# Second layer's rotated scores: query parts stacked on 128 partitions, two passes in place of three

## The chip, the cores and the metric

The kernel runs on one core of a Trainium2 chip, as one program of some 27,500 instructions on five engines: TensorE (PE in the profile; its weight loads are listed apart as PEld), VectorE (DVE), ScalarE (ACT), GpSimd (POOL) and SyncE (SP), which issues the loads of weights. The metric is the device time of one execution in microseconds (us); lower is better.

## The reference, cut to what matters

The reference is a block of two layers followed by a second block. The first layer's mixer is a gated delta rule, the second layer's is latent attention (MLA) of 256 tokens over 512 keys, 256 of the context and 256 of the sequence itself; the second block has sparse, dilated and cross attention and an MLP. All numbers are float32. The change touches the latent attention only:

```
z_lat = h_lat @ w_in                       # 384 query, 256 key/value, 64 rotary columns
ckv, kr = split(kv_part, [256])            # kr: 64 columns, shared by all 8 heads
kv = (rms_norm(ckv, g) @ w_ukv)            # per head: kn (128) and v (128)
q  = (rms_norm(cq, g) @ w_uq)              # per head: qn (128) and qr (64, rotated)
s  = einsum('bqhd,bkhd->bhqk', qn, kn) + einsum('bqhd,bkd->bhqk', qr, kr)
p  = softmax(s * 192 ** -0.5)
o  = einsum('bhqk,bkhd->bqhd', p, v)
y  = o @ w_out
```

The rotation (`rot`) is applied to qr and to the 256 keys of the sequence; the keys of the context are taken as they are.

## The kernel before, in words

**Three passes for a product.** Every float32 operand of a product is split into a high part, rounded to TensorE's input type (F32R in the code), and a low part, the remainder; ScalarE writes the high part (line 344) and VectorE the low one (line 345), in `split`. A product is then three passes of TensorE over the same accumulator: high by high, low by high, high by low (`mm3`, line 368; the fourth is left out). All passes are issued by line 366, so that the profile has them under one line and tells them apart by their tiles.

**The second layer** (`layer1`, line 1429) comes about half way through. First the keys' and queries' inputs are projected and normalised. The rotary key part is a tile `kz` of 128 partitions in which the same 64 rows stand twice (the weight columns are doubled on the host); its first 256 columns (context) are split as they are, the others after `rope` (line 1388), into `krh` and `krl`. Then come the values (`w_uv`), the rotary query parts (`ev_qr`, line 1490: for each pair of heads one tile of 128 partitions, even head on the lower 64, odd head on the upper 64, rotated and split into `qrh` and `qrl`), and, head by head, the plain query and key parts (`qk`, line 1499).

**The loop over the 8 heads** (line 1509) does for each head: the `qk` of the next head (15 passes), and for each of two tiles of 128 queries the scores of 512 keys in one PSUM bank `ps_s`: three passes with `qn`/`kn` over 128 rows and three with `qr`/`kr` over the 64 rows of this head. Then softmax (line 1406: maximum on VectorE, exponential on ScalarE, reciprocal and product on VectorE), four transposes of the result into `ps_pt`, a split of them, and 12 passes with the values into `ps_po`. There are two banks for `ps_s`, two for `ps_mm`, two for `ps_pt` and one for `ps_po`.

**What sets the order.** The instructions are recorded in program order, and a scheduler then places them on each engine by priorities and its own estimate of when each is ready; it puts passes of several heads between each other. Each engine works through its own list in that order and waits at the first instruction whose inputs are not there. Loads of weights are issued by SyncE in one queue (line 350) into a ring of buffers.

Of the kernel before, what the change touches and what calls it, by code (L numbers as in the profile page):

```python
# [10 lines left out]
F32 = mybir.dt.float32  # L11
F32R = mybir.dt.float32r
I32 = mybir.dt.int32
AF = mybir.ActivationFunctionType
ALU = mybir.AluOpType
# [4 lines left out]
P = 128  # L20
# [242 lines left out]
class K:  # L263
# [1121 lines left out]
        x["DT"] = DT  # L1385


    def rope(self, pool, z, rot, srot, cos, sin, hi, lo, T=256):

        nc = self.nc  # L1390
        p1 = self.sm()
        n = z.shape[0]
        self.mm(p1[:, :T], srot[:n], z, True, True)
        a = self.t(pool, [P, 256], "ra", 2)
        b = self.t(pool, [P, 256], "rb", 2)
        if rot is None:
            nc.gpsimd.tensor_tensor(a, z, cos, op=ALU.mult)
        else:
            p2 = self.sm()
            self.mm(p2[:, :T], rot[:n], z, True, True)  # L1400
            nc.vector.tensor_tensor(a, p2[:, :T], cos, op=ALU.mult)
        nc.vector.tensor_tensor(b, p1[:, :T], sin, op=ALU.mult)
        nc.vector.tensor_tensor(a, a, b, op=ALU.add)
        self.split(a, hi, lo)

    def softmax(self, pool, ps, n, scale, bias=None, w=256):
# [22 lines left out]
    def layer1(self):  # L1429
        nc, d = self.nc, self.d  # L1430
        m = self.mods[1]
        halves = ((0, 256), (256, 512))
        with ExitStack() as es:
            pool = es.enter_context(self.pool("mla"))
            c2 = self.consts(pool, "c2")
            qch, qcl = self.pair(pool, [P, 3, 256], "qc")
            ckh, ckl = self.pair(pool, [P, 2, 512], "ck")
            krh, krl = self.pair(pool, [P, 512], "kr")
            with self.pool("mla_l", side="right") as lp, self.pool("mla_h", side="right") as hp:
                A = self.scales(1, 1, "n1_1")  # L1440
                hl, bcs, ends = [], [], ()
                for h in (1, 0):
                    self.nrt = NRT[h]
                    hl.append(self.pair((hp, lp)[h], [P, 8, 258], f"h{h}"))
                    bcs.append(self.prepb(lp, [self.x[:, k, 256 * h:256 * h + 256] for k in range(8)],
                                          lambda k: A[:, k, 1 - h:2 - h], m[:, 0:8, 1 - h:2 - h], *hl[-1], soon=h == 1))
                    ends = ends or (self.rooted, self.spread)

                def ev(dst, ps, i):

                    b = self.t(hp, [P, 1], "zb", 4)
                    nc.vector.tensor_copy(b, ps[:, 256:257])
                    nc.vector.tensor_tensor(dst, ps[:, :256], bcs[i], op=ALU.mult)
                    nc.scalar.activation(dst, dst, AF.Identity, bias=b)

                def both(chunks, dst):

                    ws = [[w.rearrange("p (k m) -> p k m", k=8) for w in self.chunk(ap)] for ap in chunks]
                    for i, o in ((0, 256), (1, 0)):
                        for j, (wh, wl) in enumerate(ws):  # L1460
                            ps = self.ps()
                            for k in range(8):
                                self.mm3(ps[:, :258], (wh[:, k], wl[:, k]), (hl[i][0][:, k], hl[i][1][:, k]), k == 0, k == 7)
                            ev(dst(j)[:, o:o + 256], ps, i)
                cz = self.t(hp, [P, 2, 512], "cz")
                both([d["w_mc"][j] for j in range(2)], lambda j: cz[:, j])
                self.nrt = NRT[2]
                self.norm(hp, [cz[:, j] for j in range(2)], 512, lambda k, h: self.v("mkg", k),
                          None, ckh, ckl, ((0, 512),))
                kz = self.t(hp, [P, 512], "kz")  # L1470
                both([d["w_mkr"][0]], lambda j: kz)
                self.split(kz[:, :256], krh[:, :256], krl[:, :256])
                self.rope(pool, kz[:, 256:], None, c2["perm64"], c2["axc"], c2["axs"], krh[:, 256:], krl[:, 256:])
                qz = self.t(hp, [P, 3, 256], "qz")
                with self.behind(*ends):
                    self.gemm([d["w_mq"][j] for j in range(3)], 8, P, *hl[0], 258, lambda j, ps: ev(qz[:, j], ps, 0))
                self.nrt = NRT[3]
                self.norm(hp, [qz[:, j] for j in range(3)], 256, lambda k, h: self.v("mqg", k),
                          None, qch, qcl, ((0, 256),))
                self.nrt = "nr"  # L1480
                self.fill(FILL[0])
            self.mo = self.pool("mla_o", side="right")
            pool = self.mo.__enter__()
            oh, ol = self.pair(pool, [P, 8, 256], "o")
            tmp = self.pool("mla2", side="right")
            pool = tmp.__enter__()
            qrh, qrl = self.pair(pool, [P, 4, 256], "qr")
            vh, vl = self.pair(pool, [P, 4, 1024], "v")

            def ev_qr(j, ps):  # L1490
                z = self.t(pool, [P, 256], "z", 2)
                nc.scalar.activation(z, ps, AF.Copy)
                self.rope(pool, z, None, c2["perm64"], c2["axc"], c2["axs"], qrh[:, j], qrl[:, j])
            for c in range(2):
                self.gemm_tm([d["w_uv"][c]], 2, 2, ckh, ckl, 4,
                             lambda t, ps: self.split(ps, vh[:, t, c * 512:c * 512 + 512], vl[:, t, c * 512:c * 512 + 512]))
            self.gemm([d["w_uqr"][j] for j in range(4)], 3, P, qch, qcl, 256, ev_qr)

            def qk(h):
                qn, kn = self.pair(pool, [P, 256], "qn", 2), self.pair(pool, [P, 512], "kn", 2)  # L1500
                self.gemm([d["w_uqn"][h]], 3, P, qch, qcl, 256, lambda j, ps: self.split(ps, *qn))
                self.gemm([d["w_ukn"][h]], 2, P, ckh, ckl, 512, lambda j, ps: self.split(ps, *kn))
                return qn + kn
            nxt = qk(0)
            self.outer(nr=1)
            self.psum(mm=2, s=2, pt=2, po=1)
            for h in range(8):
                qnh, qnl, knh, knl = nxt
                self.fill(FILL[1])
                if h < 7:  # L1510
                    nxt = qk(h + 1)
                b = 64 * (h % 2)
                pts = [self.ps("pt"), self.ps("pt")]
                for t in range(2):
                    s = slice(t * P, (t + 1) * P)
                    ps = self.ps("s")
                    self.mm3(ps, (qnh[:, s], qnl[:, s]), (knh, knl), True, False)
                    self.mm3(ps, (qrh[b:b + 64, h // 2, s], qrl[b:b + 64, h // 2, s]), (krh[b:b + 64], krl[b:b + 64]),
                             False, True)
                    p = self.softmax(pool, ps, 512, 192.0 ** -0.5, w=512)  # L1520
                    for k in range(4):
                        self.tr(pts[k // 2][:, (k % 2) * 256 + t * P:(k % 2) * 256 + t * P + P], p[:, k * P:(k + 1) * P])
                pths = []
                for i in range(2):
                    pth = self.pair(pool, [P, 512], "pt", 4)
                    self.split(pts[i], *pth)
                    pths.append(pth)
                po = self.ps("po")
                for k in range(4):
                    q = slice((k % 2) * 256, (k % 2) * 256 + 256)  # L1530
                    self.mm3(po[:, :256], (vh[:, k, h * P:h * P + P], vl[:, k, h * P:h * P + P]),
                             (pths[k // 2][0][:, q], pths[k // 2][1][:, q]), k == 0, k == 3)
                self.split(po[:, :256], oh[:, h], ol[:, h])

            tmp.__exit__(None, None, None)
        return oh, ol
# [402 lines left out]
```

## Time and profile before

| what | value |
|---|---|
| device time, median of 3 runs (lowest, highest) | 1601.41 us (1600.74, 1604.13) |
| the profiled execution, device time | 1601.92 us |
| its span, from the first to the last instruction | 1600.1 us |
| mean granted TensorE clock, share of full speed | 0.974 |
| busy share of the span: PE, PEld, DVE, ACT, POOL | 96%, 83%, 71%, 49%, 13% |
| the loop over the 8 heads, from its first score pass to the first pass of the output product | 816.31 to 882.99 us |

The profiled execution took 0.51 us more than the median of the runs, and 1.82 us of its time lie outside the span. A pass of TensorE is listed with its start and a modelled duration; as passes are pipelined, they overlap in the list, and what a pass costs is the time from its start to the start of the next one. The loop over the heads is 4% of the span.

### The profile page before, as it was taken

What the parts mean: (1) busy time and instruction counts of PE and PEld (TensorE: products, weight loads), DVE (VectorE), ACT (ScalarE), POOL (GpSimd) and SP (SyncE); (2) the same over time, 40 slices, a digit from 0 to 9 for tenths busy, and PEclk for the clock granted to TensorE, in tenths of its full rate; (3) what the DMA queues carried; (4) which work ended last, traced back from release to release, by engine and by line L of the source; (5) the groups of instructions that cost most, each with busy time, mean ns of one, the idle gap of its engine ahead of it and who ended that gap; (6) DMA issues with size and microseconds to landing.
All of it is one profiled execution on the core that took longest, in us unless ns stands there. A gap on an engine that the chain in (4) does not pass through costs nothing.

```text
span 1600.1 us, 27482 instructions
## 1 busy us (share of the span) xinstructions
PE 1543.2 (96%) x10518; PEld 1325.5 (83%) x10518; DVE 1137.7 (71%) x2418; ACT 778.1 (49%) x1418; POOL 203.8 (13%) x191
## 2 busy tenths in 40 slices
PE   7999889999999999999999999999999999999997
PEld 4767667888888888888777799998898898889996
DVE  4556854567999895875677688988798666655655
ACT  4377733445432342354555555656445555454443
POOL 0412100100120110110000011212332010001111
PEclk9999985899999999999999999999999999999998
DMA  8356532324556674634122356564545245346553
GB/s 343 115 201 188 167 84 78 101 106 151 170 184 217 217 237 147 203 115 150 39 63 91 122 169 191 175 196 151 183 137 168 70 134 184 109 145 192 188 183 105
DMA packets 97268, 246.74 MB, mean 154 GB/s; under 512 B 25328, under 2 KB 38512, under 8 KB 96624
## 3 DMA queue, kind: packets, MB, share of 16 engines
q1 hardware_dynamic: 96848, 244.45, 47.4%
q8 instruction: 83, 1.36, 0.3%
q10 hardware_dynamic: 288, 0.52, 0.1%
q14 instruction: 49, 0.40, 0.1%
HBM read 236.82 MB, written 8.13 MB: 153 GB/s over the span
## 4 chain that ended last, share of the span: by engine, by line
PE 87%; DVE 5%; DMA 4%; ACT 3%; issue 1%; SPq 1%; ACTq 0%; DVEq 0%
PE ps_mm L366 51%; PE ps_dn L366 17%; PE ps_nr L366 4%; PE ps_s L366 4%; PE ps_su L366 3%; PE ps_po L366 2%; PE ps_lv L366 1%; DVE wlo L345 1%; DMA rawa<-in_ada 1%; PE ps_pt L389 1%; ACT whi L344 1%; PE ps_ad L366 1%; DMA kvl<-kvd 1%; PE ps_kv L366 1%; DMA raw<-in_w_qkvg 1%
## 5 line engine op out<-in xcount | busy, mean ns | idle before, releaser
L344 ACT ACTIVATE whi<-raw 128x1024 fp32r<-128x1024 f32 (+2 forms) x345 | 345.2, 1008 | 416.6 <-PE ps_mm L366 214.7
L345 DVE TENSOR_TENSOR wlo<-raw,whi 128x1024 fp32r<-128x1024 f32 (+2 forms) x334 | 397.2, 1195 | 148.3 <-ACT whi L344 146.3
L366 PE MATMUL ps_mm<-fh,whi 128*128 128x258 f32 (+2 forms) x728 | 241.4, 333 | 2.5 <-ACT fh L513 1.5
L366 PE MATMUL ps_mm<-fh,wlo 128*128 128x258 f32 (+2 forms) x728 | 240.9, 332 | 0.0
L366 PE MATMUL ps_mm<-fl,whi 128*128 128x258 f32 (+2 forms) x728 | 240.8, 331 | 0.0
L366 PEld LDWEIGHTS ps_mm<-fh,whi 128*128 128x128 f32 x728 | 137.8, 190 | 15.6 <-ACT fh L513 1.8
L366 PEld LDWEIGHTS ps_mm<-fh,wlo 128*128 128x128 f32 x728 | 137.4, 189 | 13.3 <-issue 0.4
L366 PEld LDWEIGHTS ps_mm<-fl,whi 128*128 128x128 f32 x728 | 137.9, 190 | 12.7
L813 POOL TENSOR_TENSOR act<-cg,cu 128x512 f32<-128x512 f32 (+1 forms) x44 | 76.3, 1734 | 464.3 <-DVE cu L751 313.9
L366 PE MATMUL ps_dn<-ah,whi 128*128 128x256 f32 (+1 forms) x366 | 115.9, 319 | 1.6 <-ACT whi L344 1.2
L366 PE MATMUL ps_dn<-ah,wlo 128*128 128x256 f32 (+1 forms) x366 | 115.6, 318 | 0.1
L366 PE MATMUL ps_dn<-al,whi 128*128 128x256 f32 (+1 forms) x366 | 115.2, 316 | 0.0
L676 DVE CUSTOM_DVE_ANT_0 junk<-rawa,cb,vec 128x1024 f32<-128x1024 f32 x80 | 112.5, 1406 | 0.6
L366 PEld LDWEIGHTS ps_dn<-ah,whi 128*128 128x128 f32 x366 | 68.5, 188 | 8.9 <-ACT whi L344 2.4
L366 PEld LDWEIGHTS ps_dn<-ah,wlo 128*128 128x128 f32 x366 | 68.7, 188 | 6.1 <-DVE wlo L345 0.5
L366 PEld LDWEIGHTS ps_dn<-al,whi 128*128 128x128 f32 x366 | 68.7, 188 | 4.6
L366 PE MATMUL ps_mm<-hml,whi 128*128 128x256 f32 x256 | 72.5, 283 | 0.0
L366 PE MATMUL ps_mm<-hmh,wlo 128*128 128x256 f32 x256 | 72.4, 283 | 0.0
L366 PE MATMUL ps_mm<-hmh,whi 128*128 128x256 f32 x256 | 72.3, 283 | 0.0
L366 PE MATMUL ps_mm<-hh,whi 128*128 128x256 f32 (+1 forms) x224 | 65.7, 295 | 2.1 <-DVE z L1717 1.7
L366 PE MATMUL ps_mm<-hl,whi 128*128 128x256 f32 (+1 forms) x224 | 64.2, 288 | 0.0
L366 PE MATMUL ps_mm<-hh,wlo 128*128 128x256 f32 (+1 forms) x224 | 63.8, 286 | 0.0
(648 smaller groups left out, 3865.5 us busy)
## 6 DMA issues: line engine op xcount, KB each, us to landing
raw<-in_up SPq DMA_DIRECT2D x88, 512.0 KB, 3.6
rawa<-in_adt SPq DMA_DIRECT2D x56, 512.0 KB, 4.3
rawa<-in_ada SPq DMA_DIRECT2D x40, 512.0 KB, 7.8
raw<-in_dn SPq DMA_DIRECT2D x40, 448.0 KB, 3.3
raw<-in_w_u SPq DMA_DIRECT2D x32, 512.0 KB, 3.5
raw<-in_w_d SPq DMA_DIRECT2D x32, 512.0 KB, 4.3
raw<-in_w_qkvg SPq DMA_DIRECT2D x16, 512.0 KB, 3.9
raw<-in_dn SPq DMA_DIRECT2D x16, 512.0 KB, 3.5
```

The lines of the kernel that those rows point to most:

```text
L344: self.nc.scalar.activation(hi, src, AF.Copy)
L345: (eng or self.nc.vector).tensor_tensor(lo, src, hi.bitcast(F32), op=ALU.subtract)
L366: self.nc.tensor.matmul(out, lhsT, rhs, start=start, stop=stop, **kw)
L389: self.nc.tensor.transpose(out, in_, self.ident[:in_.shape[0], :in_.shape[0]])
L676: self.nc.vector.tensor_tensor_reduce(o, r, self.cb[:, c], 1.0, self.v(f"ada_b{l}", i), ALU.mult, ALU.add, m[:, i, c:c + 1])
L813: nc.gpsimd.tensor_tensor(a, cg, cu, op=ALU.mult)
```

## The change

The two low-order passes with the rotary parts become one. A tile `qr` of 128 partitions and 8 slots, one per head, holds a head's high part on that head's own 64 partitions and its low part on the other 64. `krh` stays as it is: since the key rows stand twice, one pass of all 128 rows of `qr[h]` against `krh` gives high by high and low by high at once. For the remaining high by low there are two key tiles, `kr0` for even heads and `kr1` for odd ones, which hold the low key part on that head's half and zeros on the other half (two memsets on GpSimd); a pass of `qr[h]` against it adds high by low alone. `rope` can now return the rotated tile without splitting it.

```diff
@@ rope
-    def rope(self, pool, z, rot, srot, cos, sin, hi, lo, T=256):
+    def rope(self, pool, z, rot, srot, cos, sin, hi=None, lo=None, T=256):
...
+        if hi is None:
+            return a
         self.split(a, hi, lo)
@@ layer1, keys
-            krh, krl = self.pair(pool, [P, 512], "kr")
+            krh, *krl = [self.t(pool, [P, 512], n, 1, F32R) for n in ("krh", "kr0", "kr1")]
+            LOW = (slice(0, 64), slice(64, P))
+            for b in range(2):
+                nc.gpsimd.memset(krl[b][LOW[1 - b]].bitcast(F32), 0.0)
+
+            def keys(a, s):
+                nc.scalar.activation(krh[:, s], a, AF.Copy)
+                for b in range(2):
+                    r = LOW[b]
+                    nc.vector.tensor_tensor(krl[b][r, s], a[r], krh[r, s].bitcast(F32), op=ALU.subtract)
...
-                self.split(kz[:, :256], krh[:, :256], krl[:, :256])
-                self.rope(pool, kz[:, 256:], None, c2["perm64"], c2["axc"], c2["axs"], krh[:, 256:], krl[:, 256:])
+                keys(kz[:, :256], slice(0, 256))
+                keys(self.rope(pool, kz[:, 256:], None, c2["perm64"], c2["axc"], c2["axs"]), slice(256, 512))
@@ layer1, queries
-            qrh, qrl = self.pair(pool, [P, 4, 256], "qr")
+            qr = self.t(pool, [P, 8, 256], "qr", 1, F32R)
...
-                self.rope(pool, z, None, c2["perm64"], c2["axc"], c2["axs"], qrh[:, j], qrl[:, j])
+                a = self.rope(pool, z, None, c2["perm64"], c2["axc"], c2["axs"])
+                for b in range(2):
+                    h, r = 2 * j + b, LOW[b]
+                    nc.scalar.activation(qr[r, h], a[r], AF.Copy)
+                    nc.vector.tensor_tensor(qr[LOW[1 - b], h], a[r], qr[r, h].bitcast(F32), op=ALU.subtract)
@@ layer1, scores
-                b = 64 * (h % 2)
...
-                    self.mm3(ps, (qrh[b:b + 64, h // 2, s], qrl[b:b + 64, h // 2, s]), (krh[b:b + 64], krl[b:b + 64]),
-                             False, True)
+                    self.mm(ps, qr[:, h, s], krh, False, False)
+                    self.mm(ps, qr[:, h, s], krl[h % 2], False, True)
```

In the built program TensorE has 16 passes fewer, VectorE 6 instructions more, ScalarE 4 more and GpSimd 2 more; the order of the loads on SyncE is the same. Outside `layer1` every engine's list is the same up to the numbers in the tiles' names. Inside it the scheduler has placed some instructions anew. The first place is the first head's scores on TensorE; `ps_s_1758` and `ps_s_1762` are the banks of its two query tiles. Before:

```order
L366 MATMUL ps_s_1758_8269<-knh_1732_8187,qnh_1730_8185 128x512
L366 MATMUL ps_s_1758_8269<-knl_1733_8188,qnh_1730_8185 128x512
L366 MATMUL ps_s_1758_8269<-knh_1732_8187,qnl_1731_8186 128x512
L366 MATMUL ps_s_1758_8269<-krh_1550_7414,qrh_1680_7989 128x512
L366 MATMUL ps_s_1758_8269<-krl_1551_7415,qrh_1680_7989 128x512
L366 MATMUL ps_s_1758_8269<-krh_1550_7414,qrl_1681_7990 128x512
L366 MATMUL ps_s_1762_8288<-knh_1732_8187,qnh_1730_8185 128x512
```

And now, in the same place:

```order
L366 MATMUL ps_s_1758_8281<-knh_1732_8199,qnh_1730_8197 128x512
L366 MATMUL ps_s_1758_8281<-knl_1733_8200,qnh_1730_8197 128x512
L366 MATMUL ps_s_1758_8281<-knh_1732_8199,qnl_1731_8198 128x512
L366 MATMUL ps_s_1758_8281<-krh_1550_7414,qr_1681_7994 128x512
L366 MATMUL ps_s_1758_8281<-kr0_1551_7415,qr_1681_7994 128x512
L366 MATMUL ps_s_1762_8299<-knh_1732_8199,qnh_1730_8197 128x512
```

Five passes in a row take the place of six, and each of the five reads tiles of full height (the size at a row's end is that of the output, which does not tell the height). The second place is the fourth head's second query tile on TensorE, bank `ps_s_1843`, where before two transposes into `ps_pt_1810` stood among the rotary passes:

```order
L366 MATMUL ps_s_1843_8588<-knh_1800_8432,qnl_1799_8431 128x512
L366 MATMUL ps_s_1843_8588<-krh_1550_7414,qrh_1680_7989 128x512
L389 MATMUL ps_pt_1810_8467<-c0_61,p_1813_8476 128x128 x2
L366 MATMUL ps_s_1843_8588<-krl_1551_7415,qrh_1680_7989 128x512
L366 MATMUL ps_s_1843_8588<-krh_1550_7414,qrl_1681_7990 128x512
```

Now the same bank has:

```order
L366 MATMUL ps_s_1839_8575<-kr1_1552_7416,qr_1681_7994 128x512
L366 MATMUL ps_po_1797_8423<-pth_1793_8415,vh_1682_7995 128x256
L366 MATMUL ps_s_1843_8593<-knh_1800_8440,qnh_1798_8438 128x512
L366 MATMUL ps_s_1843_8593<-knl_1801_8441,qnh_1798_8438 128x512
L366 MATMUL ps_s_1843_8593<-knh_1800_8440,qnl_1799_8439 128x512
L366 MATMUL ps_s_1843_8593<-krh_1550_7414,qr_1681_7994 128x512
L366 MATMUL ps_s_1843_8593<-kr1_1552_7416,qr_1681_7994 128x512
```

The transposes have moved behind the scores. Before, three of the 16 score banks were filled with other work among their rotary passes; one is now. The third place is on VectorE, ahead of the loop: `knl_1733` is the low key part of the first head, `ra` and `rb` are the two halves of a rotation, `wlo` the low part of a weight, and `qrl` or `qr` the low part of a pair of heads' rotary queries. Before:

```order
L345 TENSOR_TENSOR qrl_1681_7990<-ra_1704_8097,qrh_1680_7989 128x256
L345 TENSOR_TENSOR wlo_1750_8237<-raw_1748_8234,whi_1749_8236 128x384
L1402 TENSOR_TENSOR rb_1713_8125<-ps_dn_1711_8122,c2_7408 128x256
L1403 TENSOR_TENSOR ra_1712_8124<-ra_1712_8124,rb_1713_8125 128x256
L345 TENSOR_TENSOR wlo_1754_8255<-raw_1752_8252,whi_1753_8254 128x256
L345 TENSOR_TENSOR qnl_1731_8186<-ps_mm_1737_8195,qnh_1730_8185 128x256
L1402 TENSOR_TENSOR rb_1721_8152<-ps_dn_1719_8149,c2_7408 128x256
L345 TENSOR_TENSOR qrl_1681_7990<-ra_1712_8124,qrh_1680_7989 128x256
L1403 TENSOR_TENSOR ra_1720_8151<-ra_1720_8151,rb_1721_8152 128x256
L345 TENSOR_TENSOR wlo_1777_8337<-raw_1775_8334,whi_1776_8336 128x384
L1402 TENSOR_TENSOR rb_1729_8179<-ps_dn_1727_8176,c2_7408 128x256
L345 TENSOR_TENSOR knl_1733_8188<-ps_mm_1741_8213,knh_1732_8187 128x512
```

Now:

```order
L1510 TENSOR_TENSOR qr_1681_7994<-ra_1704_8101,qr_1681_7994 64x256 x2
L1402 TENSOR_TENSOR rb_1713_8131<-ps_dn_1711_8128,c2_7408 128x256
L345 TENSOR_TENSOR wlo_1750_8249<-raw_1748_8246,whi_1749_8248 128x384
L1403 TENSOR_TENSOR ra_1712_8130<-ra_1712_8130,rb_1713_8131 128x256
L345 TENSOR_TENSOR wlo_1754_8267<-raw_1752_8264,whi_1753_8266 128x256
L345 TENSOR_TENSOR qnl_1731_8198<-ps_mm_1737_8207,qnh_1730_8197 128x256
L1402 TENSOR_TENSOR rb_1721_8160<-ps_dn_1719_8157,c2_7408 128x256
L1510 TENSOR_TENSOR qr_1681_7994<-ra_1712_8130,qr_1681_7994 64x256 x2
L1403 TENSOR_TENSOR ra_1720_8159<-ra_1720_8159,rb_1721_8160 128x256
L345 TENSOR_TENSOR wlo_1777_8347<-raw_1775_8344,whi_1776_8346 128x384
L1402 TENSOR_TENSOR rb_1729_8189<-ps_dn_1727_8186,c2_7408 128x256
L345 TENSOR_TENSOR knl_1733_8200<-ps_mm_1741_8225,knh_1732_8199 128x512
```

Ahead of `knl_1733` stand two instructions more, as each of two `qrl` of 128 partitions has become a pair of 64; otherwise one `rb` and one `wlo` have changed places.

## Rows read from the trace of the kernel before

**Rows 1.** Busy time by stretch of the loop; columns as in the second line.

```profile
core 0: us, PE busy (x) PEld busy (x) DVE busy (x) ACT busy (x) POOL busy (x), PEclk, DMA share, GB/s
815.00:865.00 50.00, 50.00 (x268) 37.38 (x268) 37.53 (x89) 29.67 (x67) 0.00 (x0) 1.00 0.25 76
865.00:885.00 20.00, 17.51 (x104) 12.99 (x104) 12.82 (x33) 7.89 (x19) 0.00 (x0) 1.00 0.22 61
```

**Rows 2.** DVE groups by shape, 814 to 890: busy, mean ns, idle before.

```profile
L1416 DVE TENSOR_REDUCE mx<-ps_s 128x1 f32<-128x512 f32 x16 | 11.0, 688 | 7.4 <-PE ps_s L366 7.4
```

**Rows 3.** PE in order of time, first head: start us, us, engine, tiles, rows*columns.

```profile
816.31 0.39 PE L366 MATMUL ps_s<-knh,qnh 128*128 128x512 f32 x1
816.54 0.40 PE L366 MATMUL ps_s<-knl,qnh 128*128 128x512 f32 x1
816.77 0.40 PE L366 MATMUL ps_s<-knh,qnl 128*128 128x512 f32 x1
817.10 0.50 PE L366 MATMUL ps_s<-krh,qrh 64*128 64x512 f32 x1
817.44 0.39 PE L366 MATMUL ps_s<-krl,qrh 64*128 64x512 f32 x1
817.67 0.39 PE L366 MATMUL ps_s<-krh,qrl 64*128 64x512 f32 x1
817.99 0.50 PE L366 MATMUL ps_s<-knh,qnh 128*128 128x512 f32 x1
818.33 0.39 PE L366 MATMUL ps_s<-knl,qnh 128*128 128x512 f32 x1
```

**Rows 4.** PEld in order of time, same place; idle before in brackets.

```profile
816.55 0.19 PEld L366 LDWEIGHTS ps_s<-knh,qnl 128*128 128x128 f32 x1
817.10 0.18 PEld L366 LDWEIGHTS ps_s<-krh,qrh 64*128 64x128 f32 x1 [0.37 <-issue]
```

**Rows 5.** PE and PEld groups by shape, 814 to 890.

```profile
L366 PE MATMUL ps_s<-krh,qrh 64*128 64x512 f32 x16 | 8.0, 499 | 0.0
...
L366 PEld LDWEIGHTS ps_s<-krh,qrh 64*128 64x128 f32 x16 | 2.9, 183 | 5.4 <-issue 5.3
```

**Rows 6.** PE in order of time, ahead of the loop.

```profile
813.76 0.39 PE L366 MATMUL ps_mm<-qch,whi 128*128 128x256 f32 x1 [1.86 <-DVE knl L345]
```

**Rows 7.** DVE in order of time, ahead of the loop.

```profile
815.51 0.43 DVE L345 TENSOR_TENSOR wlo<-raw,whi 128x256 fp32r<-128x256 f32 x1 [0.23 <-ACT whi L344]
815.85 0.42 DVE L345 TENSOR_TENSOR qnl<-ps_mm,qnh 128x256 fp32r<-128x256 f32 x1
```

**Rows 8.** Groups by shape on 64 partitions, whole span, one for each engine.

```profile
L1384 DVE TENSOR_SCALAR DT<-ps_lv 64x256 f32<-64x256 f32 x6 | 2.5, 422 | 4.2 <-PE ps_lv L366 4.2
...
L1379 ACT ACTIVATE X<-ps_lv 64x256 f32<-64x256 f32 x6 | 2.3, 378 | 3.7 <-PE ps_lv L366 3.5
...
L1350 POOL MEMSET D<- 64x256 f32 x8 | 2.4, 305 | 38.6 <-PE ps_lv L366 31.4 <-PE ps_mm L366 3.6 <-PE ps_s L366 3.5
```

**Rows 9.** DVE, first layer: three instructions on different partitions in a row.

```profile
219.84 0.90 DVE L1368 TENSOR_SCALAR DT<-ps_lv 32x128 f32<-32x128 f32 x3
```

**Rows 10.** POOL in order of time, start of the second layer.

```profile
744.51 1.50 POOL L551 TENSOR_TENSOR sqs<-x 128x256 f32<-128x256 f32 x1 [38.40 <-DMA c<-in_c]
```

**Rows 11.** DVE in order of time, behind the key parts' splits.

```profile
779.14 0.16 DVE L1452 COPY zb<-ps_mm 128x1 f32<-128x1 f32 x1 [2.20 <-PE ps_mm L366]
```

**Rows 12.** What PE waited for, 865 to 885: us, times, longest.

```profile
PE ps_po L366 <- ACT pth L344: 1.5, 3, 0.5
PE ps_po L366 <- DVE ptl L345: 0.7, 2, 0.3
```

**Rows 13.** Busy time by stretch, ahead of the values' product.

```profile
789.00:794.00 5.00, 4.60 (x12) 3.71 (x13) 3.89 (x9) 2.46 (x6) 0.00 (x0) 0.57 0.00 0
```

**Rows 14.** Softmax of the first head's second tile: DVE's maximum.

```profile
819.88 0.69 DVE L1416 TENSOR_REDUCE mx<-ps_s 128x1 f32<-128x512 f32 x1 [0.90 <-PE ps_s L366]
```

**Rows 15.** The same on ACT: the sum's reading behind the exponential.

```profile
822.23 0.20 ACT L1418 ACTIVATION_READ_ACCUMULATOR p<-ps_s,mx 128x1 f32 x1
```

## The prediction

> **What bounds the kernel now.** I read the busy time by stretch first, because the change touches 4% of the span and a mean over the whole says little. From 815 to 865 us TensorE is busy without a gap (50.00 of 50.00 us), VectorE for 37.53 and ScalarE for 29.67; from 865 to 885, with the last heads, TensorE is busy for 17.51 of 20 [rows 1]. So the first fifty microseconds are bound by the passes, and only the tail has waits. The groups of VectorE say the same from the other side: its idle time before the softmax maxima, 7.4 us over 16 of them, is time in which it waits for TensorE's scores [rows 2]. What the change saves in passes is therefore saved in time for as long as VectorE's softmax keeps up.
>
> **What one block of scores costs.** The list of TensorE's passes in order of time gives the first head's first tile. I take a pass's cost as the distance from its start to the next start, since the durations in the list overlap. The plain passes start at 816.31, 816.54 and 816.77, 0.23 us apart. Then the tiles change from 128 rows to 64: the first rotary pass starts 0.33 after its forerunner (0.10 too late), the next 0.34 after that (0.11 too late), the next 0.23, and the following block's first pass 0.32 after the last (0.09 too late); that one, of 128 rows again, takes 0.34 itself (0.11 too late) [rows 3]. The block takes 817.99 - 816.31 = 1.68 us, and the way in and out of the rotary passes costs 0.10 + 0.11 + 0.09 + 0.11 = 0.41 us beside the passes. The weight loads show why: that of a 128-row pass behind 128-row passes runs at 816.55, beside the pass that began at 816.54. That of the first 64-row pass begins only at 817.10, with its own pass, after 0.37 us of idle for which the profile names no awaited engine [rows 4]. Over 16 blocks these idle times are 5.3 us, and the first rotary pass has a mean listed duration of 499 ns where the plain ones show 390 to 400 [rows 3, 5].
>
> A rule of the Trainium skill speaks against this reading and against the change: the page "TensorE: Matmul & The Clock Gate", in its Part 3 "Packing small matmuls — row/col tiling", under "What overlaps and what doesn't", says that a weight load overlaps running passes only when the row groups differ. By it a load of full height waits until a full-height pass is through, and the two new passes would give up the cover that two heights might have had. The load at 816.55 uses the same rows as the pass beside it and overlaps it all the same, and the load that does not overlap is the one whose rows differ in part, so the trace disagrees.
>
> **The sum in the loop.** Two passes of 128 rows at 0.23, with no change of height before, between or behind them, take the place of three at 0.23 and of 0.41 us of stalls: 0.23 + 0.41 = 0.64 us for each of 16 blocks, 10.2 us. Three blocks were split by other work and so changed height once more; I take 0.2 us for each, half of the 0.41, as the other work can hide some of it: 0.6 us. Together 10.8 us, of which 3.7 are passes (16 x 0.23) and 7.1 are stalls. The bounds: if a full-height load did not run ahead, a new pass would take a load and a pass, 0.19 + 0.23 = 0.42 us [rows 3, 4]; two then cost 0.84 instead of 0.69 + 0.41 = 1.10, and 16 x 0.26 = 4.2 us remain. If the height had nothing to do with the stalls, only the 3.7 of the passes remain. I take 10.8, since the rows show plain passes behind plain passes at 0.23 throughout.
>
> **What is added ahead of the loop.** Each of two low query parts of 128 partitions has become a pair of 64, ahead of `knl_1733` on VectorE. Here TensorE waits: before the next head's first product, at 813.76, it stands idle for 1.86 us for that instruction [rows 6], so two more instructions there are on the path. A 128x256 instruction of this kind costs 815.85 - 815.51 = 0.34 us from start to start [rows 7]; at that rate the two cost 0.7. The other end: an instruction on 64 partitions with 256 columns lasts 0.42 if nothing of it overlaps [rows 8], and instructions that change partitions in the first layer follow each other at 0.90 / 3 = 0.30 us though they have half the columns [rows 9]. With no overlap for the four, and none for the one behind each pair, the price is 6 x 0.42 - 4 x 0.34 = 1.2. I take 1.0, nearer to the upper end, since the new instructions read one half of the partitions and write the other in turn, which is what the first layer's row is like. Below 0.7 I see no way: behind the two stand the same instructions as before.
>
> The Trainium skill has this as a rule: "VectorE: DVE Perf Modes", in "Two Vector instructions with no wait between them", says that an instruction is held until every earlier one has finished when it starts on another group of 32 partitions than the last read or write of that memory. By it the price would be the 1.2 of the full durations, by plain overlap the 0.7; the first layer's 0.30 for 128 columns is on the rule's side.
>
> **What is added where something hides it.** The two memsets on GpSimd, of 64x512, are some 0.6 us each by twice the 305 ns of 64x256 [rows 8]; that engine had been idle for 38.40 us before its first work in this layer [rows 10], and the zeros are read only in the loop. Without that cover they would cost 1.2 us. The four low key parts instead of two stand ahead of VectorE's 2.20 us of idle before 779.14, in which it waits for TensorE [rows 11]; two more at 0.34 to 0.42 fit. If the cover were gone they would cost 0.8. The four more ScalarE copies are 0.38 us each [rows 8] and lie where that engine is busy for little more than half of the time; bare, they would add 1.5 us, and the longer wait on TensorE is VectorE's in any case. I count all three at nothing.
>
> **The tail.** From 865 on, TensorE waits 1.5 us for `pth` and 0.7 for `ptl`, the split of the transposed softmax [rows 12]. There the last heads' softmax sets the pace, and a shorter block of scores lets it start earlier by less than the block saves. At worst all four blocks of the last two heads give nothing, 4 x 0.64 = 2.6 us; at best nothing is lost, since each maximum starts from its own block's end. I take 0.5, nearer to the best end, because only 2.5 us of the 20 are idle.
>
> **Sum.** 10.8 - 1.0 - 0.5 = 9.3 us. From the profiled execution's 1601.92 that gives 1592.6. The median of the runs is 0.51 lower, 1601.41, and it is the median that is asked for: 1592.1 us.
>
> **The rivals.**
> *VectorE becomes the bound in the middle.* 815 to 865 has 50.00 us for 37.53 us of VectorE's work. With some 8 of the 50 gone, the work is the same and the share rises from 75% to about 89%. For it: each head's maximum, exponential and product is a chain in which small waits add up. Against: 89% still leaves room, and its idle before the maxima was a wait for TensorE. I price it as the loss of a quarter of the gain, 2.5 us: 1594.6.
>
> *TensorE's clock falls at the longer wait.* Ahead of the values' product, from 789 to 794, the granted clock was 0.57 though TensorE was listed busy for 4.60 of the 5 us [rows 13], which is near the lower of its two levels, 1.2 of 2.4 GHz. Behind the 1.86 us wait it did not fall, for the passes at 816.31 run at 0.23. If a wait of 2.9 us brings such a stretch, 5 us at 0.57 lose 2.1: 1594.2.
>
> *It doesn't do what it says.* Only the passes go, 3.7 - 1.0 = 2.7: 1598.7; or the loads don't run ahead, 4.2 - 1.0 = 3.2: 1598.2. For it speaks only that a rotary pass against a full-height key tile isn't in the trace; against it are all the plain passes.
>
> *Slower: the two score banks hold TensorE up.* A bank is free for the next head once the exponential has read it: from the maximum's start at 819.88 to the end of the sum's reading, 822.23 + 0.20, 2.55 us [rows 14, 15]. Between two uses of a bank TensorE now has the other tile's five passes (5 x 0.23 = 1.15) and the next head's 15 (816.31 - 813.76 = 2.55), 3.7 us. The rival decides from a chain longer than 3.7 us, and it eats the whole gain from 3.7 + 9.3 / 8 = 4.9 us. If VectorE, at 89%, lets maxima queue up behind products and splits so that the chain grows to 5.4, TensorE loses 1.7 us in each of 8 heads, 13.6: 1605.7. Against it: the measured chain is 1.15 us short of the limit.
>
> **How the numbers follow.** Forecast 0.73, with its own range 1590 to 1594.3 (front price 0.7 to 1.2, tail loss 0 to 2.6, split blocks 0 to 2 us). VectorE as the bound 0.14, the clock 0.05, the rival in which little is saved 0.05, the banks 0.03. Faster or slower is counted from 0.2% on, 3.2 us, about what a measurement of this kernel can tell from no change; the bounds are 1598.2 and 1604.6. Forecast, VectorE and clock lie on the faster side: 0.92. The case of little saved lies at 1598.2 and above: same, 0.05. The banks: slower, 0.03. The range 1590.0 to 1596.0 takes in the forecast's own and the middle of the next two cases.
>
> **What would show it.** Right: the rotary passes as 128*128 rows, each 0.23 us from the next, in blocks of 1.15; no idle before their weight loads; TensorE's wait before 813.76's pass grown from 1.86 to about 2.9; the loop, from the first score pass to the first pass of the output product, at some 56.5 us where it was 66.7; VectorE's 7.4 us of idle before the maxima shrunk. Wrong: rotary passes 0.33 or more apart; waits of TensorE for `ps_s` behind the exponential; idle for `pth` and `ptl` in the middle of the loop instead of its tail; a granted clock below 1 behind the wait.

## The result and the profile after

The changed kernel took 1592.85 us, the median of 4 runs (1590.16 to 1594.01), against 1601.3 us of the kernel before; the ratio is 0.9941, with a 95% interval of 0.9924 to 0.9959. That is 8.5 us less. The forecast was 1592.1, 1590.0 to 1596.0. The profiled execution took 1592.31 us, its span 1590.5, 9.6 us less than the span of before.

The first head's scores, in the profile of the changed kernel's second execution (called e1 below; its clock was at full speed here, which makes it comparable with [rows 3]). PE in order of time: start us, us, engine, tiles, rows*columns.

```profile
814.16 0.39 PE L366 MATMUL ps_s<-knh,qnh 128*128 128x512 f32 x1
814.39 0.40 PE L366 MATMUL ps_s<-knl,qnh 128*128 128x512 f32 x1
814.63 0.39 PE L366 MATMUL ps_s<-knh,qnl 128*128 128x512 f32 x1
814.86 0.40 PE L366 MATMUL ps_s<-krh,qr 128*128 128x512 f32 x1
815.09 0.40 PE L366 MATMUL ps_s<-kr,qr 128*128 128x512 f32 x1
815.33 0.39 PE L366 MATMUL ps_s<-knh,qnh 128*128 128x512 f32 x1
815.56 0.39 PE L366 MATMUL ps_s<-knl,qnh 128*128 128x512 f32 x1
...
870.21 0.28 PE L366 MATMUL ps_mm<-oh,whi 128*128 128x256 f32 x1
```

The weight loads of the next block, same kernel and columns, to be read beside these passes and [rows 4]:

```profile
815.33 0.19 PEld L366 LDWEIGHTS ps_s<-knl,qnh 128*128 128x128 f32 x1
815.56 0.19 PEld L366 LDWEIGHTS ps_s<-knh,qnl 128*128 128x128 f32 x1
815.79 0.19 PEld L366 LDWEIGHTS ps_s<-krh,qr 128*128 128x128 f32 x1
816.01 0.19 PEld L366 LDWEIGHTS ps_s<-kr,qr 128*128 128x128 f32 x1
```

A block takes 815.33 - 814.16 = 1.17 us where it took 1.68 [rows 3], and its follower no longer pays for the way out. Every load starts together with the pass before its own, the rotary ones too; the 0.37 us of idle of [rows 4] is gone. The last row is the first pass of the output product, where the loop ends.

What the change added shows ahead of the loop. TensorE's wait for `knl`, in the profile of the changed kernel's first execution (PE in order of time; idle before and what ended it in brackets):

```profile
812.16 0.58 PE L366 MATMUL ps_mm<-qch,whi 128*128 128x256 f32 x1 [3.14 <-DVE knl L345]
...
814.24 0.63 PE L366 MATMUL ps_mm<-ckh,whi 128*128 128x512 f32 x1
814.67 0.63 PE L366 MATMUL ps_mm<-ckl,whi 128*128 128x512 f32 x1
...
818.04 0.40 PE L366 MATMUL ps_s<-krh,qr 128*128 128x512 f32 x1
818.27 0.40 PE L366 MATMUL ps_s<-kr,qr 128*128 128x512 f32 x1
```

The wait is 3.14 us where it was 1.86 [rows 6]. Behind it the passes of 512 columns start 0.43 us apart, and from 818.04 on 0.23: TensorE ran at about the lower of its two levels, 1.2 in place of 2.4 GHz. The stretches show it, with the granted clock in the column behind the five engines (busy us, count). The changed kernel's first execution:

```profile
784.00:796.00 12.00, 9.64 (x49) 7.70 (x49) 9.11 (x28) 5.82 (x12) 0.00 (x0) 1.00 0.06 16
811.00:819.00 8.00, 6.84 (x23) 5.84 (x24) 5.42 (x13) 3.86 (x8) 0.00 (x0) 0.57 0.16 42
```

The kernel before, in the same two places:

```profile
786.00:798.00 12.00, 10.36 (x37) 7.98 (x37) 7.17 (x19) 5.05 (x11) 0.00 (x0) 0.72 0.00 0
811.00:819.00 8.00, 6.14 (x30) 4.18 (x29) 6.47 (x15) 4.72 (x9) 0.84 (x1) 1.00 0.26 73
```

The clock fell once in either profile, but in another place: ahead of the values' product before [rows 13], behind the wait for `knl` after. One profile of each kernel cannot say whether the change moved it there.

**The ledger.** Four passes can be found in every profile: the second values' product (the `whi,ckh` pass behind a wait of about 0.73 us for `vl`), the first `qn` pass behind the wait for `knl`, the first score pass, and the first pass of the output product. The time between them leaves out the first layer, where executions differ: a pass ahead of the change's place, the first `h1h,whi` behind a wait for `cz`, starts between 761.45 and 769.75 us in the profiles of this case.

| us | values to `qn` | `qn` to scores | the loop | sum | clock fell |
|---|---|---|---|---|---|
| before | 16.10 | 2.55 | 66.68 | 85.33 | ahead of the values |
| after, first execution | 17.38 | 4.64 | 56.61 | 78.63 | behind the wait |
| after, second execution (e1) | 17.37 | 2.56 | 56.05 | 75.98 | ahead of the values |

The first and the last row have their fall of the clock ahead of this stretch, so they can be compared: 16.10 to 17.37 is +1.27 for the front, 66.68 to 56.05 is -10.63 for the loop, and the sum is -9.35 us. The middle row pays for its fall inside the stretch (2.08 us in the 15 passes, 0.56 at the loop's start), but saves the other: from the norm's passes `c,rq` to the second values' product it took 794.78 - 785.03 = 9.75 us, and before 797.66 - 785.80 = 11.86, which is 2.11 more.

**The output.** The two kernels do not give the same numbers. The kernel before agrees with the reference (e8 below, and e7 in another order); the output of the changed kernel has a relative error of 0.060 (e1 and e11, the same kernel, and e4, e6, e9 and e10 with the same figure). Two runs leave the low query part times the high key part out, one with passes of 64 rows (e3), one with zeros in its place in the stacked tile (e5): both have 0.106, the same to every digit. That points to the low query parts in the stacked pass, whose product with the high keys would then come out less fully than in a pass of its own; it is not shown, and why is open. What follows is about time, and the saving is not shown at equal accuracy.

### The profile page after: what moved, and what is told of

Read it like the earlier page. It is cut to its first block, busy times and chain, and to the rows that moved or that the text cites. A ratio compares the mean times of both kernels' runs of the same rounds, so it can differ in the third digit from the quotient of the medians.

```text
span 1590.5 us, 27460 instructions
## 1 busy us (share of the span) xinstructions
PE 1533.2 (96%) x10502; PEld 1325.4 (83%) x10502; DVE 1140.6 (72%) x2424; ACT 779.5 (49%) x1422; POOL 204.8 (13%) x193
## 4 chain that ended last, share of the span: by engine, by line
PE 86%; DVE 5%; DMA 4%; ACT 3%; issue 1%; SPq 0%; ACTq 0%; DVEq 0%
PE ps_mm L366 51%; PE ps_dn L366 17%; PE ps_nr L366 4%; PE ps_s L366 4%; PE ps_su L366 3%; PE ps_po L366 1%; PE ps_lv L366 1%; DVE wlo L345 1%; DMA rawa<-in_ada 1%; PE ps_ad L366 1%; PE ps_pt L389 1%; ACT whi L344 1%; PE ps_kv L366 1%; DMA raw<-in_w_qkvg 1%; DMA kvl<-kvd 1%
```

## The experiments

Theory: the saving is the loop's, some 3.7 us of passes and 7 us of stalls where the height of the tiles changes; against it stand the low query parts on VectorE. Rivals: the number of passes alone makes the gain; the extra wait makes the clock fall, and so costs more than itself. Each run is timed against the kernel before on its own chip; the places named are those of the ledger, since single executions of one kernel differ by more than most of the edits (e1's twelve lie between 1575.5 and 1595.1 us).

**e1_again, e8_before_again and e11_again_b: both kernels again, nothing edited.**

> The changed kernel once more, nothing altered. In its first profile TensorE's granted clock fell behind the 3.14 us wait for `knl` (passes of 512 columns 0.43 us apart from 814.24 to 817.66, where they are 0.23 later). Theory: the longer wait brings the fall, so it is there again, at the same pass, and the time is 1592.9 within 1.5 us. Rival: where the clock falls is a matter of the single execution; then the fall is elsewhere or gone (some 2.7 us less in that stretch), and the wait stays at 3.1 us.

> The kernel before once more, nothing altered, for the place where TensorE's clock falls. In the profiles so far it fell once in this layer: either ahead of the values' product (787 to 794) or behind the wait for `knl`. If the 3.1 us wait is what can bring the second kind, this kernel with its 1.86 us shows the first kind or none; if the place is free, it can fall behind the 1.86 us wait too.

> The changed kernel once more, on the chip of these runs, to compare with. The loop at TensorE's full clock is 56.0 us, the stretch from the second value product to the first pass behind the wait 17.4 us, the wait 3.1 us; the clock falls once in the layer, at one of two places.

Measured: e1 1592.37 us against 1601.15 (ratio 0.9943, 0.9917 to 0.9970); e11 1594.37 against 1603.18 (0.9942, 0.9921 to 0.9963); e8 1602.16 against 1602.16 (0.9994, 0.9973 to 1.0016). In e1 the clock fell ahead of the values' product, in e11 behind the wait again. And in the kernel before, e8, it fell behind the wait of 1.86 us this time:

```profile
784.00:794.00 10.00, 7.84 (x38) 6.11 (x38) 7.33 (x20) 5.22 (x11) 0.00 (x0) 1.00 0.00 0
804.00:816.00 12.00, 10.14 (x45) 7.93 (x44) 8.79 (x20) 6.53 (x15) 1.91 (x2) 0.86 0.27 81
```

Its stretches are 16.09, 4.10 and 66.69 us: front and loop as before to 0.01 us, and 1.55 lost to the clock in the 15 passes. So both kernels show both places: the longer wait is neither needed for the fall behind it nor enough. Whether it makes that place likelier is not shown by so few profiles. The theory of e1's expectation, that the fall would be there again at the same pass, is wrong; its rival holds.

**e2_three_full: as many passes as before, all of full height.**

```diff
-                    self.mm(ps, qr[:, h, s], krl[h % 2], False, True)
+                    self.mm(ps, qr[:, h, s], krl[h % 2], False, False)
+                    self.mm(ps, qr[:, h, s], krl[h % 2], False, True)
```

> The changed kernel with the second rotary pass issued twice, so that a block has three rotary passes of full height (the high-by-low product is added twice, the output is not the reference's). Theory: a full-height pass behind full-height passes costs 0.23 us; 16 x 0.23 = 3.7 us more in the loop than with two: 1596.6, loop 56.6 + 3.7 = 60.3 us, still 6 us under the 66.7 of before though the count of passes is that of before. Rival (the count of passes made the gain): the time returns to 1601 and the loop to 66. Second rival (loads are not hidden): 16 x 0.42 = 6.7 us more, 1599.6.

**e3_two_half: as few passes as after, all rotary ones of 64 rows.**

```diff
-                    self.mm3(ps, (qrh[b:b + 64, h // 2, s], qrl[b:b + 64, h // 2, s]), (krh[b:b + 64], krl[b:b + 64]),
-                             False, True)
+                    self.mm(ps, qrh[b:b + 64, h // 2, s], krh[b:b + 64], False, False)
+                    self.mm(ps, qrh[b:b + 64, h // 2, s], krl[b:b + 64], False, True)
```

> The kernel before with its third rotary pass (high key part with low query part) left out, so that a block has two rotary passes, both of 64 rows (low by high is left out, the output is not the reference's). Theory: one pass of 0.23 us goes from each of 16 blocks, and the four stalls at the changes of height stay, 0.41 us a block: 1601.3 - 3.7 = 1597.6, loop 63.0 us; the first rotary pass still starts 0.33 us after its forerunner. Rival (the count made the gain): 10 us less, 1591, loop 56.6.

Measured: e2 1594.24 us, e3 1597.53, both against 1601.15 (ratios 0.9951, 0.9921 to 0.9982, and 0.9961, 0.9918 to 1.0004). By these times e3 cannot be told from no change, so the loops decide: 877.61 - 818.17 = 59.44 us and 880.86 - 817.21 = 63.65 us. e2's loop, its first and last row:

```profile
818.17 0.39 PE L366 MATMUL ps_s<-knh,qnh 128*128 128x512 f32 x1
...
877.61 0.28 PE L366 MATMUL ps_mm<-oh,whi 128*128 128x256 f32 x1
```

e3's first block, PE in order of time:

```profile
817.67 0.40 PE L366 MATMUL ps_s<-knh,qnl 128*128 128x512 f32 x1
818.00 0.50 PE L366 MATMUL ps_s<-krh,qrh 64*128 64x512 f32 x1
818.34 0.39 PE L366 MATMUL ps_s<-krl,qrh 64*128 64x512 f32 x1
818.65 0.50 PE L366 MATMUL ps_s<-knh,qnh 128*128 128x512 f32 x1
818.99 0.39 PE L366 MATMUL ps_s<-knl,qnh 128*128 128x512 f32 x1
```

All four stalls are still there with two passes: 0.33, 0.34, 0.31 and 0.34 us where a plain pass takes 0.23. But e3's loop is not all at the full clock. Near its end TensorE fell to the lower level once more, as it did nowhere in the loops of before, e1 and e2 (granted clock in the column behind the five engines):

```profile
860.00:890.00 30.00, 27.45 (x173) 22.79 (x172) 20.67 (x49) 15.59 (x35) 0.00 (x0) 0.94 0.28 88
...
869.73 0.41 PE L366 MATMUL ps_po<-pth,vl 128*128 128x256 f32 x1
869.94 0.41 PE L366 MATMUL ps_po<-pth,vh 128*128 128x256 f32 x1
```

From 869.32 on its passes of 256 columns start 0.21 us apart where it is 0.12 elsewhere. Set against the same kinds of pass at the full clock, the stretch up to 872.85 lost about 1.5 us, an estimate; without it e3's loop would be some 62.15. The two kernels and the two originals make a square:

| loop, us | three passes | two passes |
|---|---|---|
| rotary tiles of 64 rows | 66.68 (before) | 63.65 (e3); about 62.15 at the full clock |
| rotary tiles of 128 rows | 59.44 (e2) | 56.05 (e1) |

At the full clock a pass fewer saves about 4.5 or 3.39 us, the full height 7.24 or about 6.1. Each is one profile, but a loop at the full clock repeats to 0.01 us (66.68, 66.69 and 66.69 in before, e7 and e8; 56.05 and 56.04 in e1 and e5). Some 57 to 68% of the gain are the height, and the rival of the count falls. A full-height pass costs 3.39 / 16 = 0.21 us, so its load is hidden. The Trainium skill, in "TensorEngine Tiling (Array Packing)", section "Key Properties", says that a change of the tiling mode drains TensorE, without a price. The trace agrees that such a change costs time, 6.1 to 7.24 us for 16 blocks here, 0.38 to 0.45 for a way in and out.

**e4_low_pool: the low query parts on GpSimd.**

```diff
-                    nc.vector.tensor_tensor(qr[LOW[1 - b], h], a[r], qr[r, h].bitcast(F32), op=ALU.subtract)
+                    nc.gpsimd.tensor_tensor(qr[LOW[1 - b], h], a[r], qr[r, h].bitcast(F32), op=ALU.subtract)
```

> The changed kernel with the eight subtractions for the low query parts on GpSimd in place of VectorE; TensorE's order is the same. Theory: four instructions of 0.45 us go from VectorE's queue ahead of `knl`, so TensorE's wait there falls from 3.14 to about 1.3 us, and the clock does not fall behind it: 1592.9 - 1.8 - 2.7 = 1588.4. Rival 1: the fall of the clock does not hang on this wait: 1592.9 - 1.8 = 1591.1. Rival 2: GpSimd is slower (0.75 us for 128x256 there) and the rotation's products behind it come late, so that `knl` waits for them: no gain, 1592.9 or more.

Measured: 1593.2 us against 1601.15 (0.9945, 0.9910 to 0.9980); the stretches are 17.11, 4.64 and 56.73, the wait 2.88 us. Only 0.26 us of the 1.27 came back, so the theory's 1.8 failed. Rows of VectorE and GpSimd in the same stretch show why:

```profile
808.10 0.42 DVE L1402 TENSOR_TENSOR rb<-ps_dn,c 128x256 f32<-128x256 f32 x1 [0.76 <-PE ps_dn L366]
808.48 1.08 DVE L345 TENSOR_TENSOR wlo<-raw,whi 128x384 fp32r<-128x384 f32 x1
```

```profile
807.60 1.54 POOL L1510 TENSOR_TENSOR qr<-ra,qr 64x256 fp32r<-64x256 f32 x2 [1.02 <-ACT qr L1509]
```

Where a GpSimd product had begun first, a VectorE instruction of two inputs in SBUF mostly took up to twice as long: `wlo` of 128x384 1.08 us, where the kernel before shows one of 0.56 that began ahead of GpSimd's. GpSimd beside two other such `wlo`, first in the changed kernel's first execution (`wlo` at 810.09), then in the kernel before (at 811.88; both stand further below):

```profile
809.79 0.96 POOL L1397 TENSOR_TENSOR ra<-z,c 128x256 f32<-128x256 f32 x1 [2.73 <-DVE qr L1510]
811.51 0.84 POOL L1397 TENSOR_TENSOR ra<-z,c 128x256 f32<-128x256 f32 x1 [1.69 <-DVE qrl L345]
```

All three `wlo` end 0.42 us after the GpSimd instruction that was running: 809.56 after 809.14, 811.17 after 810.75, 812.77 after 812.35. So what they lost is what was left of GpSimd's instruction when they began. What left VectorE's queue came back as slower instructions, and 0.76 us of waiting for the rotation's pass with it. Rival 2 saw the missing gain, but named another way to it.

**e5_one_low: one instruction for a pair's low parts.**

```diff
+            qx = self.t(pool, [P, 4, 256], "qx", 1, F32R)
+            for h in range(8):
+                nc.gpsimd.memset(qr[LOW[1 - h % 2], h].bitcast(F32), 0.0)
...
-                    nc.vector.tensor_tensor(qr[LOW[1 - b], h], a[r], qr[r, h].bitcast(F32), op=ALU.subtract)
+                nc.vector.tensor_tensor(qx[:, j], a, qr[:, 2 * j].bitcast(F32), op=ALU.subtract)
```

> The changed kernel with the low query parts written by one VectorE instruction of 128 partitions for a pair of heads, to a tile that nothing reads, and zeros in their place in `qr` (low by high is left out; the output is not the reference's). All passes stay. Theory (the front's price is the two pairs held on VectorE at 0.45 us an instruction, 1.1 to 1.3 us): TensorE's wait for `knl` falls from 3.13 back to about 1.9 us, the loop stays at 56.05 us, and the stretch from the second value product to the first `qn` pass behind the wait from 17.37 to 16.1. Rival (the wait grew because ScalarE or GpSimd delivers the rotations later): the wait stays above 2.8.

Measured: 1593.25 us against 1602.16 (0.9953, 0.9936 to 0.9969); stretches 16.31, 4.08 and 56.04, wait 2.07. So 1.06 of the 1.27 us hang on splitting two instructions into four, the theory holds but for 0.21 us, and the loop is the changed kernel's. Its median lies 8.9 us below that of before, e1's 8.8, so a median tells nothing of this edit; here the clock fell behind the wait, for 1.5 us.

**e6_qk_first and e7_before_qk_first: the first head's products ahead of the rotary ones,** in the changed kernel and in the one before.

```diff
-            self.gemm([d["w_uqr"][j] for j in range(4)], 3, P, qch, qcl, 256, ev_qr)
...
             nxt = qk(0)
+            self.gemm([d["w_uqr"][j] for j in range(4)], 3, P, qch, qcl, 256, ev_qr)
             self.outer(nr=1)
```

> The changed kernel with the first head's plain query and key products ahead of the rotary query products, in place of behind them. Theory (TensorE waits there only because `knl` stands behind the rotations on VectorE): the 3.13 us wait for `knl` goes; what is left is a wait of the first scores for the rotary parts, up to 1.5 us; so 1.6 to 3.1 us less: 1592.4 - 2.3 = 1590.1. Rival: VectorE is the engine that is full there (4.7 of 5 us), so the same work delays the first scores by as much: 1592.4.

> The same change of order in the kernel before. Theory: its 1.86 us wait for `knl` goes or shrinks, so 0.5 to 1.9 us less than before: 1601.2 - 1.2 = 1600.0; and the distance to the changed kernel in this order is the loop's alone, 10.6 us. Rival as for the changed kernel: 1601.2, with another wait in the place of this one.

Measured: e6 1592.57 us and e7 1600.27, both against 1602.16 (0.9943, 0.9926 to 0.9960, and 0.9998, 0.9980 to 1.0016). From the second values' product to the first score, e6 takes 17.65 us (e1 19.93) and e7 17.06 (before 18.65); the loops are 57.63 (56.05) and 66.69 (66.68). The wait for `knl` goes in both. In the kernel before its 1.59 us stay saved; in the changed one 1.58 of 2.28 us come back in the loop, which now has these two waits:

```profile
PE ps_mm L366 <- DVE knl L345: 1.4, 1, 1.4
...
PE ps_mm L366 <- DVE qnl L345: 0.7, 1, 0.7
```

That is near e6's rival, VectorE being full, though what is late are the next head's projections and not the first scores: with shorter score blocks, TensorE reaches them before VectorE has cleared its queue. The gain left is 0.70 us, not the 2.3 expected. The distance between e7 and e6 is 8.5 us in these stretches, not the 10.6 expected. Neither gain shows in the medians.

**e9_two_late and e10_three_late: rotary products of later heads inside the loop.** The edit for two; e10 has `range(1)` and `h + 1`, `1 <= j`.

```diff
-            self.gemm([d["w_uqr"][j] for j in range(4)], 3, P, qch, qcl, 256, ev_qr)
+            self.gemm([d["w_uqr"][j] for j in range(2)], 3, P, qch, qcl, 256, ev_qr)
...
                     nxt = qk(h + 1)
+                j = h + 2 - 1
+                if 2 <= j < 4:
+                    self.gemm([d["w_uqr"][j]], 3, P, qch, qcl, 256, lambda _, ps: ev_qr(j, ps, "mm"))
```

> The changed kernel with the rotary query products of pairs 2 and 3 (heads 4 to 7) taken out of the stretch ahead of the loop and put into its first two steps, beside the scores of heads 0 and 1 (their rotation uses a bank of the projections there). Theory (VectorE is full ahead of the loop and has some 3 us in 40 free inside it): the 3.1 us wait for `knl` shrinks below 1.5, the loop grows by the 18 passes and two rotations moved, 2.3 us, and 1.5 to 3 us are gained in sum: 1590 where the changed kernel has 1592.4. Rival (inside the loop VectorE is as good as full): the loop grows by 4 us or more, with waits for `ptl` or `p`, and nothing is gained.

> The same with three pairs inside the loop and only the first ahead of it. Theory: as with two, and no wait for `knl` of the first head is left; the loop grows by 27 passes, 3.4 us; time within 1 us of the kernel with two. Rival: VectorE in the loop is full, the loop grows by 6 us or more, and the time is that of the changed kernel or above.

Measured, with e11 on the same chip (1594.37 us): e9 1590.44 (0.9911, 0.9881 to 0.9941), e10 1594.07 (0.9935, 0.9920 to 0.9950), before 1603.18. From the second values' product to the first score e9 takes 14.99 us, the loop 59.88, in sum 74.87; e10 12.03, its loop 62.84, in sum 74.87 as well. Against e1's 75.98 both gain 1.11 us: the front's 4.9 and 7.9 us less are paid back in the loop but for that. For e9 the theory had 2.3 us more in the loop and 1.5 to 3 gained, the rival 4 or more and nothing; the 3.83 and 1.11 measured lie between. For e10 the loop grew by 6.79 us, as its rival said, yet the stretches gain as much as with two. Most of e9's growth is the moved work itself, 18 passes and four more of the rotations. Its waits in the loop are 3.6 us where e1's are 2.8, which makes up 0.8 of the 3.83; the two longest are new:

```profile
PE ps_pt L389 <- DVE mx L1419: 1.5, 1, 1.5
PE ps_pt L389 <- DVE rs L1421: 1.2, 1, 1.2
```

Here, near the loop's end, TensorE waits for the softmax's small VectorE instructions. e9 has the lower median, but its interval and e11's (0.9921 to 0.9963) overlap: that it beats the changed kernel is likely by its trace, and not shown by its times.

## Why the prediction was right

**The loop.** Forecast 10.8 less 0.5, so 10.3 us; measured 10.63. The split into 3.7 of passes and 7.1 of stalls is measured as 3.4 and 7.2 by way of e2, and as about 4.5 and 6.1 by way of e3. VectorE's share from 815 to 865 was put at 89%. In e1, columns as before:

```profile
814.00:864.00 50.00, 48.84 (x300) 42.68 (x298) 44.70 (x108) 33.06 (x78) 0.00 (x0) 1.00 0.32 97
```

44.70 of 50.00 us are 89%. VectorE's idle before the maxima went from 7.4 us [rows 2] to 0.8 in e1:

```profile
L1418 DVE TENSOR_REDUCE mx<-ps_s 128x1 f32<-128x512 f32 x16 | 10.9, 684 | 0.8 <-PE ps_s L366 0.7
```

So VectorE came near to being the bound: it lost nothing here, but part of what e6 and e9 moved came back as waits for it.

**The front.** Forecast 1.0, bounds 0.7 and 1.2; measured 1.27, a little above the upper end. VectorE in the changed kernel's first execution:

```profile
805.37 0.87 DVE L1510 TENSOR_TENSOR qr<-ra,qr 64x256 fp32r<-64x256 f32 x2 [0.15 <-ACT qr L1509]
806.27 0.42 DVE L1402 TENSOR_TENSOR rb<-ps_dn,c 128x256 f32<-128x256 f32 x1
...
808.84 0.87 DVE L1510 TENSOR_TENSOR qr<-ra,qr 64x256 fp32r<-64x256 f32 x2
809.74 0.42 DVE L1403 TENSOR_TENSOR ra<-ra,rb 128x256 f32<-128x256 f32 x1
810.09 1.08 DVE L345 TENSOR_TENSOR wlo<-raw,whi 128x384 fp32r<-128x384 f32 x1
811.09 0.41 DVE L1402 TENSOR_TENSOR rb<-ps_dn,c 128x256 f32<-128x256 f32 x1
```

In the kernel before, in the same place:

```profile
808.24 0.43 DVE L345 TENSOR_TENSOR qrl<-ra,qrh 128x256 fp32r<-128x256 f32 x1 [0.15 <-ACT qrh L344]
808.66 0.56 DVE L345 TENSOR_TENSOR wlo<-raw,whi 128x384 fp32r<-128x384 f32 x1
...
811.03 0.41 DVE L345 TENSOR_TENSOR qrl<-ra,qrh 128x256 fp32r<-128x256 f32 x1
811.36 0.41 DVE L1403 TENSOR_TENSOR ra<-ra,rb 128x256 f32<-128x256 f32 x1
811.88 0.89 DVE L345 TENSOR_TENSOR wlo<-raw,whi 128x384 fp32r<-128x384 f32 x1
812.69 0.41 DVE L1402 TENSOR_TENSOR rb<-ps_dn,c 128x256 f32<-128x256 f32 x1
```

A pair takes 0.90 us to the next start, in place of one instruction of 0.42 and one of 0.33: +0.48 and +0.57. The step of `wlo` grew from 0.81 to 1.00, +0.19: it now begins 0.66 us ahead of the end of GpSimd's product, where it was 0.47 before. By the ends compared under e4 that is the reason; it was not tried by itself. That is 1.24 of the 1.27; the last term was not in the sum. The rule of the Trainium skill that the prediction weighed ("VectorE: DVE Perf Modes", "Two Vector instructions with no wait between them") has the trace's agreement here: at 0.45 us a step, these instructions do not overlap.

**The tail.** Forecast a loss of 0.5 against a full saving. Its waits went from 2.5 us [rows 1, 12] to these, in the changed kernel's first execution:

```profile
PE ps_po L366 <- ACT pth L344: 1.3, 3, 0.5
PE ps_s L366 <- ACT p L1420: 0.8, 1, 0.8
PE ps_po L366 <- DVE ptl L345: 0.7, 2, 0.3
```

2.8 us, so 0.3 were lost. The wait for `p`, a score bank not yet read, was 0.3 us in the kernel before. It is the slower rival in small, once and not in every head: in e1 the first head's maxima start at 816.07 and the second sum is read by 819.21, 3.14 us for both tiles together, under the limit of 3.7.

**What cost nothing.** The low key parts stand between the `h1h,whi` pass named above and the norm's `c,rq`: 20.87 us before, 20.90 after. In the ledger nothing but front and loop moved, and no wait for the memsets' zeros or ScalarE's copies shows in it.

**The clock.** The prediction took from one execution that the clock did not fall behind the 1.86 us wait, and made the longer wait its condition. That step failed: e8 has the fall behind the shorter wait. In the changed kernel's first execution the fall did come behind the longer one; it cost 2.64 us there, near the rival's price of 2.1, and saved 2.11 ahead of the values' product. It did no harm to the sum, because in most profiles one fall is paid in one of the two places. What decides the place is open; e10 had none in either.

**Luck.** The front cost 0.27 us more than forecast and the loop gave 0.33 more: they cancel. The forecast's own range is also narrower than its terms: a front of 1.2, a tail loss of 2.6 and nothing for the split blocks give 1595.0 at the upper end, not 1594.3. The stated range of 1590.0 to 1596.0 holds that too.

## What to carry to other kernels

Read a pass's price from the starts of a row of equal passes, and compare it with the starts around a pass of another height: the difference is what a change to full tiles gives, and here it was one and a third to two times the pass that was saved. Compare the outputs before stacking a high and a low part in one pass: here the error rose to 0.060. Zeros in the unused half of an operand cost no TensorE time if the pass is as long anyway; placing data on other partitions costs VectorE a full instruction for each half. Where an engine stands at 89%, part of a second gain on the engine it feeds is handed back as waits: of e6's 2.28 us 1.58 came back.

## What was not expected of the hardware

- In 13 profiles of this case the clock fell in this layer ahead of the values' product in seven, behind the wait for `knl` in five, and in neither place in one, at a price of about 1.5 to 2.6 us, with both places seen for the kernel before and for the changed one. One of the seven, e3, had a second fall inside the loop. Two profiles of one kernel must be set beside each other by stretches at the same clock.
- A GpSimd product that began first held a VectorE subtraction of two inputs in SBUF until it was through (three of 128x384 end 0.42 us after it, and one took 1.08 us in place of 0.56), so that moving 64x256 subtractions to GpSimd, at about 0.8 us each, gave back 0.26 us of 1.27.
